# Two column blocks of the gate product at a time as seven half-size products (Strassen-Winograd) in a fused decoder layer

## The chip, the cores and the metric

One core of a Trainium2 chip runs the whole kernel as one program; the other cores are not used. The metric is the device time of one execution in microseconds. Every time in this document is of that program or of a variant of it with the same inputs.

## The reference, cut to what matters

One decoder layer on x, 512 rows of 1024, in float32. Three branches (dilated attention, a gated spatial mix, cross-attention into 256 memory rows) are each projected to 1024 channels, weighted by gates made from x, summed and projected once more; a gated MLP follows. The change is in the gates.

```python
gates = jax.nn.sigmoid((x @ w_gate + b_gate).astype(jnp.float32)).reshape(b_, s_, N_BRANCH, D_MODEL)
merged = (gates[:, :, 0] * (oa @ w_proj_a) + gates[:, :, 1] * (ob @ w_proj_b)
          + gates[:, :, 2] * (oc @ w_proj_c))
y = merged.astype(x.dtype) @ w_out
```

`w_gate` is 1024 x 3072: 24 column blocks of 128, eight to a branch.

## The kernel before, in words

**Products in three passes.** TensorE multiplies in a reduced float32 format. Every operand is therefore held as a high and a low part, and each product is made of three matmuls (`mm3`, L218 to L220): low weights with high data, high weights with low data, high with high. Each matmul loads its 128 x 128 weights anew. Nearly all matmuls stand at L220.

**The weight stream.** `add_load` (L99) lists the loads of weights, in the order of their use, and cuts each into units of up to 1024 columns. `emit_load` (L108) issues one load of up to 1 MB from SP's queue into one of three `raw` tiles. `emit_split` (L119) splits one unit: ScalarE writes the high part (`wh`, L133), VectorE the low part (`wl`, L134); there are four tiles of each (`wspl`). `unit()` (L141) hands out the next unit and first emits the splits of the two behind it and the loads of the two behind its own.

**The gates** (L780 to L795). For each of 24 blocks, a unit of 8 x 128 weights and 24 matmuls of 512 columns (8 row blocks of the weights, three passes) make `gate` in one PSUM bank; x stands transposed and split in `xTh` and `xTl`. ScalarE makes tanh of it (`gt`, L791). `merge` (L762) then multiplies the branch's projection for that block: 6 or 12 matmuls into `proj`, weights from a unit that serves four blocks (branches 0 and 2) or two (branch 1), and VectorE's L770, or L772 and L773, and in branch 2 also the split of the merged block (`mTh` L775, `mTl` L776). The merge of a block stands behind the gate matmuls of the next one (`late`).

**Beside it.** A generator, `side()` (L608), holds the attention, the spatial gating and the cross-attention in small steps; `fill()` (L621) takes one step, and stands behind every six gate matmuls. At the gates' start the spatial gating and the cross-attention are still to be done; they last into the first quarter of the gates.

**The order of the work.** The program text gives each instruction a priority. A scheduler, at compile time, sets the order in each engine's queue from these and from when operands and tiles should be ready, so that a later instruction can be put ahead of an earlier one; on the chip each engine runs its queue in order. Tiles come from pools: `big` (17 tiles of 8 KB a partition, `T8`), `work` (6 of 2 KB, `W2`), `raw` (3), `wspl` (4 and 4), PSUM (8 banks). An instruction that writes a new tile waits until one is free.

**After the gates.** `project` (L816) multiplies by `w_out`: two steps of 24 matmuls for all rows, then the last six steps for each row block in turn, with weights that `last_rows` (L798) splits into six `big` tiles (`lh`, `ll`). A norm, the MLP and a second norm follow.

Of the kernel before, what the change touches and what calls it, by code (L numbers as in the profile page):

```python
# [11 lines left out]
F32 = mybir.dt.float32  # L12
F32R = mybir.dt.float32r
AF = mybir.ActivationFunctionType
ALU = mybir.AluOpType
# [34 lines left out]
def bucket_rows():  # L50
    """Per dilation group the bucket (one-hot, rows 0-31) and the mask (row 32) of each diagonal."""
    rows = np.zeros((N_BUCKETS + 1, 3, VW), np.float32)
    for i in range(VW):
        for g in range(3):
            n = 255 - i if g == 0 else 127 - i
            if g == 0:
                ok, dist = 0 <= n <= 128, n
            elif g == 1:
                ok, dist = n >= 0, 4 * n
            else:  # L60
                ok, dist = n >= 0 and n % 4 == 0, 4 * n
            if ok:
                rows[int(bucket_of(np.array([dist]))[0]), g, i] = 1.0
            else:
                rows[N_BUCKETS, g, i] = NEG
    return rows
# [3 lines left out]
def layer_kernel(  # L70
# [8 lines left out]
    wspl = ctx.enter_context(tc.tile_pool(name="wspl", bufs=4))  # L79
    work = ctx.enter_context(tc.tile_pool(name="work", bufs=6))  # L80
    small = ctx.enter_context(tc.tile_pool(name="small", bufs=4))
# [11 lines left out]

    # ---------------------------------------------------------------- weight stream
    loads, prepared = [], {}
# [3 lines left out]
    def add_load(shape, src, parts):  # L99
        """One DMA of `shape`; parts: function raw -> list of (hi shape, raw view)."""  # L100
        n = len(loads)
        loads.append((shape, src))
        for f in parts:
            units.append((n, f))

    raws = {}

    def emit_load():  # L108
        n = state["load"]
        if n >= len(loads):  # L110
            return
        shape, src = loads[n]
        t = wraw.tile([P, 2048], F32, tag="raw", name=f"raw{n}")
        v = t[:, :shape[1] * shape[2]].rearrange("p (a b) -> p a b", a=shape[1])
        nc.sync.dma_start(v, src)
        raws[n] = v
        state["load"] += 1

    def emit_split():  # L119
        u = state["split"]  # L120
        if u >= len(units):
            return
        n, f = units[u]
        while state["load"] <= n:
            emit_load()
        src = f(raws[n])
        a = src.shape[1]
        h = wspl.tile([P, 1024], F32R, tag="wh", name=f"wh{u}")
        l = wspl.tile([P, 1024], F32R, tag="wl", name=f"wl{u}")
        size = a * src.shape[2]  # L130
        h3 = h[:, :size].rearrange("p (a b) -> p a b", a=a)
        l3 = l[:, :size].rearrange("p (a b) -> p a b", a=a)
        nc.scalar.activation(h3, src, AF.Copy)  # L133
        nc.vector.tensor_tensor(l3, src, h3.bitcast(F32), op=ALU.subtract)  # L134
        prepared[u] = (h3, l3)
        state["split"] += 1

    AHEAD = 2
    cursor = {"u": 0}

    def unit():  # L141
# [7 lines left out]
        return prepared.pop(u)  # L149

    def cols2(w, c0):
        src = w[:, c0:c0 + 256].rearrange("(k p) c -> p k c", p=P)
        add_load([P, 8, 256], src, [lambda r: r[:, :, 0:128], lambda r: r[:, :, 128:256]])

    def kcols(w, k0, nk, c0, nc_):
        """Rows k0*128.., a [128, nk, nc_] load in units of 1024 per partition."""
        src = w[k0 * P:(k0 + nk) * P, c0:c0 + nc_].rearrange("(k p) c -> p k c", p=P)
        per = 1024 // nc_
        parts = [lambda r, s=s: r[:, s:s + per, :] for s in range(0, nk, per)]
        add_load([P, nk, nc_], src, parts)  # L160
# [17 lines left out]
    kcols(wkv, 0, 8, 256, 256)  # L178
    for half in range(2):
        add_load([P, 2, 512], w_proj_a[0][:, half * 512:half * 512 + 512].rearrange("(k p) c -> p k c", p=P),  # L180
                 [lambda r: r])
        for j in range(2):
            cols2(wgate, half * 512 + 256 * j)
    for q in range(4):
        add_load([P, 4, 256], w_proj_b[0][:, q * 256:q * 256 + 256].rearrange("(k p) c -> p k c", p=P),
                 [lambda r: r])
        cols2(wgate, 1024 + q * 256)
    for half in range(2):
        add_load([P, 2, 512], w_proj_c[0][:, half * 512:half * 512 + 512].rearrange("(k p) c -> p k c", p=P),
                 [lambda r: r])  # L190
        for j in range(2):
            cols2(wgate, 2048 + half * 512 + 256 * j)
    def krows(w, k, split):
# [20 lines left out]
    def mm3_ops(ps, w, v, first, last):  # L214
        """ps += w.T @ v for operands split into (hi, lo)."""
        return ((ps, w[1], v[0], first, False), (ps, w[0], v[1], False, False), (ps, w[0], v[0], False, last))
# [11 lines left out]

    # ---------------------------------------------------------------- x, transposed and split
    xraw = []  # L230
# [39 lines left out]

    # ---------------------------------------------------------------- small parameters
    rows = const.tile([P, P], F32, name="rows")
# [60 lines left out]

    # ---------------------------------------------------------------- q, k, v
    qk12 = [T8(f"qk{i}") for i in range(2)]
# [85 lines left out]

    # ---------------------------------------------------------------- attention pieces
    NM = const.tile([P, 48], F32, name="NM")
# [3 lines left out]
    class Pair:  # L427
        """Two query blocks of one head: scores, softmax, weighted values (transposed)."""

# [7 lines left out]
        def score_ops(self):  # L437
            """Matmul arguments of the scores, in order."""
            part, h, pr = self.part, self.h, self.pr
# [80 lines left out]
    def alternate(a, b):  # L520
        """The matmuls of two heads in turn: they use different rows or columns of the array."""
        for pair in zip(a, b):
# [3 lines left out]
    def pipeline(groups):  # L526
        """groups: (part, first head, done); scores run two steps ahead of values."""
        items = [[Pair(part, h + i, pr) for i in range(2)] + [gi] for gi, (part, h, _) in enumerate(groups)
# [99 lines left out]

    # ---------------------------------------------------------------- gated spatial inputs, memory
    sgb = T8("sgb")  # L630
# [52 lines left out]
    kcT = [kct[:, i, :].rearrange("p (a c) -> p a c", a=2) for i in range(2)]  # L683
    vcN = T8("vcN")[:, 0, :].rearrange("p (a c) -> p a c", a=2)
    for j in range(2):
# [25 lines left out]
    nc.vector.tensor_copy(vcN, ps.rearrange("p (b c) -> p b c", b=2))  # L711
    ready.add("mix")

    # ---------------------------------------------------------------- spatial gating, cross-attention
    obT_h = T8("obTh", F32R)
# [32 lines left out]

    # ---------------------------------------------------------------- gates and branch projections
    m = [T8(f"m{i}") for i in range(2)]  # L750
# [27 lines left out]

    late = None
    for br, (nk, per, src) in enumerate(branches):  # L780
        for f in range(KD):
            if f % per == 0:
                wp = unit()
            w = unit()
            ps = bank("gate")
            for k in range(KD):
                mm3(ps, (w[0][:, k, :], w[1][:, k, :]), xs(k), k == 0, k == KD - 1)
                if k % 2 == 1:
                    fill()
            t = W2("gt")  # L790
            nc.scalar.activation(t, ps, AF.Tanh, bias=gb5[:, br * 8 + f:br * 8 + f + 1], scale=0.5)  # L791
            if late is not None:
                merge(*late)
            late = (br, f, t, wp)
    merge(*late)  # L795

    # ---------------------------------------------------------------- output projection, first norm
    def last_rows(n):  # L798
        """Split rows of the last LAST steps of a [*, 1024] weight, kept whole."""
        rows = []  # L800
# [15 lines left out]
    def project(nk, src, n, norm_in):  # L816
        """src (transposed, split) times the weight of the stream; norm_in(b) after each row block."""
        py = [[bank(f"y{b}{hf}") for hf in range(2)] for b in range(NB)]
# [64 lines left out]

    # ---------------------------------------------------------------- gated MLP
    h2 = [T8(f"h2_{i}", F32R) for i in range(NF // 2)]
# [36 lines left out]

    # ---------------------------------------------------------------- down projection, second norm
    lnp2 = T8("ln2").rearrange("p (k a) c -> p k (a c)", k=2)
# [25 lines left out]
```

## Time and profile before

| what | value |
|---|---|
| median of 3 runs | 822.16 us (822.1 to 822.8) |
| profiled execution, span from first to last instruction | 820.5 us |
| TensorE busy | 807.0 us (98%) |
| weight loads busy | 675.0 us (82%) |
| VectorE, ScalarE, GpSimd busy | 382.5, 284.4, 20.4 us |
| gates and projections | 211.5 to 405.3 us of the span |

The profiled execution is one run, and its own time is known by its span alone, 820.5 us; the median of the runs, 822.16, lies 1.7 us above it. An engine is busy in a row while one of its instructions is under way; TensorE's matmuls overlap, so their single durations add up to more than the time they take together, and the time of one is best read from the start of a run of them to the start of the next.

### The profile page before, as it was taken

To read this page: it belongs to the slowest core of one execution; us is meant where nothing else is said; L and a number is where in the kernel's file an instruction comes from. 1 tells how busy PE (TensorE), PEld (TensorE's weight loads), DVE (VectorE), ACT (ScalarE), POOL (GpSimd) and SP (SyncE) were. 2 spreads that over 40 slices of the span, in tenths; PEclk is the share of its full clock that TensorE was granted. 3 is DMA by queue.
4 is the path that set the end of the run, shared out by engine and by line. 5 is a ranking of instruction groups with operands and counts; after the bars stand their busy time and mean duration, and the time that the engine had idled before them with its cause. 6 is when DMAs were issued, how large, how long until landed. Compare 5 with 4: busy or idle time off the path is not lost.

```text
span 820.5 us, 9700 instructions
## 1 busy us (share of the span) xinstructions
PE 807.0 (98%) x4051; PEld 675.0 (82%) x4051; DVE 382.5 (47%) x591; ACT 284.4 (35%) x433; POOL 20.4 (2%) x32
## 2 busy tenths in 40 slices
PE   7999999999999999999999999999999999999996
PEld 6878997778877788888888988888888888888884
DVE  4333235836664334335856455544454445225055
ACT  4331246665365222223611243333333333224000
POOL 2001000100000000000000000000000000000000
PEclk9999999999999999999999999999999999999998
DMA  9355331122402133242840023233333324224002
GB/s 317 124 196 182 103 129 52 52 78 82 150 26 78 52 103 128 78 152 89 323 154 1 1 103 102 103 103 103 103 103 102 103 83 131 94 102 154 1 26 77
DMA packets 62411, 87.10 MB, mean 106 GB/s; under 512 B 1994, under 2 KB 50154, under 8 KB 62368
## 3 DMA queue, kind: packets, MB, share of 16 engines
q1 hardware_dynamic: 60960, 82.32, 29.5%
q0 software_dynamic: 1408, 4.17, 1.5%
q8 instruction: 32, 0.52, 0.3%
q14 instruction: 11, 0.09, 0.0%
HBM read 84.36 MB, written 4.47 MB: 108 GB/s over the span
## 4 chain that ended last, share of the span: by engine, by line
PE 98%; DMA 1%; DVE 0%; SPq 0%; issue 0%; DVEq 0%
PE y L220 20%; PE gate L220 16%; PE pa L220 13%; PE pb L220 13%; PE qk L220 7%; PE zb L220 6%; PE proj L220 5%; PE v L220 4%; PE up L220 3%; PE oT L524 1%; PE sc L524 1%; PE qc L220 1%; PE pt L493 1%; PE qk L362 1%; PE vc L220 1%; PE kc L220 1%
## 5 line engine op out<-in xcount | busy, mean ns | idle before, releaser
L134 DVE TENSOR_TENSOR wl<-raw,wh 128x1024 fp32r<-128x1024 f32 (+1 forms) x127 | 154.1, 1214 | 186.5 <-ACT wh L133 177.7
L133 ACT ACTIVATE wh<-raw 128x1024 fp32r<-128x1024 f32 (+1 forms) x127 | 133.2, 1050 | 192.9 <-PE pb L220 47.2
L220 PE MATMUL y<-wh,h 128*128 128x512 f32 x256 | 79.0, 389 | 0.0
L220 PE MATMUL gate<-xTh,wl 128*128 128x512 f32 x192 | 76.7, 400 | 0.0
L220 PE MATMUL gate<-xTh,wh 128*128 128x512 f32 x192 | 75.0, 390 | 0.0
L220 PE MATMUL gate<-xTl,wh 128*128 128x512 f32 x192 | 74.9, 390 | 0.0
L220 PE MATMUL pa<-hTh,wl 128*128 128x512 f32 x160 | 62.3, 389 | 0.0
L220 PE MATMUL pa<-hTl,wh 128*128 128x512 f32 x160 | 62.3, 389 | 0.0
L220 PE MATMUL pa<-hTh,wh 128*128 128x512 f32 x160 | 62.2, 389 | 0.0
L220 PE MATMUL pb<-hTh,wl 128*128 128x512 f32 x160 | 62.2, 389 | 0.0
L220 PE MATMUL pb<-hTl,wh 128*128 128x512 f32 x160 | 62.2, 389 | 0.0
L220 PE MATMUL pb<-hTh,wh 128*128 128x512 f32 x160 | 62.2, 389 | 0.0
L220 PEld LDWEIGHTS y<-wh,h 128*128 128x128 f32 x256 | 48.0, 188 | 10.1
L220 PE MATMUL y<-wl,h 128*128 128x512 f32 x128 | 49.8, 389 | 0.0
L898 DVE SCALAR_TENSOR_TENSOR c<-pa,par,c 128x511 f32<-128x511 f32 x20 | 15.0, 750 | 65.8 <-ACT c L897 65.8
L220 PEld LDWEIGHTS gate<-xTh,wl 128*128 128x128 f32 x192 | 36.1, 188 | 8.6 <-issue 1.2
L220 PEld LDWEIGHTS gate<-xTh,wh 128*128 128x128 f32 x192 | 36.0, 188 | 7.8
L897 ACT ACTIVATE c<-pa,par 128x512 f32<-128x512 f32 x20 | 15.6, 781 | 76.1 <-PE pa L220 76.1
L220 PEld LDWEIGHTS gate<-xTl,wh 128*128 128x128 f32 x192 | 36.1, 188 | 7.0
L220 PE MATMUL qk<-xTh,wl 128*128 128x512 f32 (+1 forms) x96 | 35.8, 374 | 0.0
L220 PE MATMUL qk<-xTh,wh 128*128 128x512 f32 (+1 forms) x96 | 35.7, 371 | 0.0
L220 PE MATMUL qk<-xTl,wh 128*128 128x512 f32 (+1 forms) x96 | 35.6, 372 | 0.0
(219 smaller groups left out, 1480.8 us busy)
## 6 DMA issues: line engine op xcount, KB each, us to landing
raw<-in_w_ffn_up SPq DMA_DIRECT2D x22, 1024.0 KB, 4.9
raw<-in_w_in SPq DMA_DIRECT2D x13, 1024.0 KB, 5.0
raw<-in_w_gate SPq DMA_DIRECT2D x12, 1024.0 KB, 5.0
raw<-in_w_ffn_down SPq DMA_DIRECT2D x11, 1024.0 KB, 4.7
raw<-in_w_out SPq DMA_DIRECT2D x4, 1024.0 KB, 4.7
shear<-vecs POOLq DMA_DIRECT2D x1, 2304.0 KB, 14.1
raw<-in_w_mem_kv SPq DMA_DIRECT2D x2, 1024.0 KB, 5.3
raw<-in_w_proj_b SPq DMA_DIRECT2D x4, 512.0 KB, 3.3
```

The source lines that it names most:

```text
L133: nc.scalar.activation(h3, src, AF.Copy)
L134: nc.vector.tensor_tensor(l3, src, h3.bitcast(F32), op=ALU.subtract)
L220: nc.tensor.matmul(ps, w, v, start=first, stop=last)
L362: nc.tensor.matmul(ps[:, sl], w[a][:, k, :], xs(k0 + k, sl)[c], start=k0 + i + k == 0, stop=k0 > 0 and i == 2 and k == 3)
L493: nc.tensor.transpose(pt[:, kb, u, :], self.p[:, u, kb * P:(kb + 1) * P], ident)
L524: nc.tensor.matmul(ps, w, v, start=first, stop=last)
L897: nc.scalar.activation(c, pa, AF.Identity, bias=CB(i), scale=CW(2, i))
L898: nc.vector.scalar_tensor_tensor(c[:, 1:], pa[:, :S - 1], CW(1, i), c[:, 1:], op0=ALU.mult, op1=ALU.add)
```

## The change

Blocks 0 to 3 of branch 0 stay. From block 4 on, two neighbouring blocks f and f + 1 are made together. Their weights are a 2 x 2 matrix of quarters (rows 0 to 511 and 512 to 1023 of w_gate; columns of f and of f + 1), a11, a12, a21, a22, of 4 x 128 x 128 each; x is a 2 x 2 matrix of quarters too (the same halves of its channels; rows 0 to 255 and 256 to 511). Winograd's form of Strassen's method makes the 2 x 2 product from seven products of quarters instead of eight, with sums of quarters.

- **Sums of x** (`data_sums`): made once, ahead of the gates, on GpSimd (5 instructions of 1024 columns) and VectorE (3), then split (4 on ScalarE, 4 on VectorE) into four `big` tiles that live until the last group.
- **Sums of weights**: for each load, three GpSimd instructions of 512 columns when it has landed (two into a tile of the new pool `wsum`, one in place), and a fourth in place once the load's first unit is split.
- **Units**: four a group instead of two: a11 and a12; the two sums; a11 - a21 and a22; the quarter a12 less a sum (512 columns).
- **Products** (`Seven`): each is 4 x 3 = 12 matmuls of 256 columns. In order: 1 (unit 1, into x), 2 (unit 1, into y), 3 (unit 2, added to x), 4 (unit 2, into z), 5 (unit 3, added to x), then the late merges of the group before, 6 (unit 3, added to x), 7 (unit 4, added to z). x has a PSUM bank, y and z share one. ScalarE copies x after products 1, 3 and 5; VectorE adds these copies to y and z into the two `gt` tiles after products 2, 5 and 7; ScalarE makes tanh in three parts. `fill()` stands behind each product.
- **Room**: `vcN` moves from `big` to `const`, `work` has 7 tiles, and the scratch for DMAs that GpSimd issues is set to 4096.

```diff
-    work = ctx.enter_context(tc.tile_pool(name="work", bufs=6))
+    wsum = ctx.enter_context(tc.tile_pool(name="wsum", bufs=2))
+    work = ctx.enter_context(tc.tile_pool(name="work", bufs=7))
...
+        if n in seven_loads:
+            s = wsum.tile([P, 2, 512], F32, tag="sums", name=f"sums{n}")
+            s2, s1 = [s[:, i, :].rearrange("p (k c) -> p k c", k=4) for i in range(2)]
+            a11, a21, a22 = v[:, 0:4, 0:P], v[:, 0:4, P:2 * P], v[:, 4:8, P:2 * P]
+            nc.gpsimd.tensor_tensor(s1, a21, a22, op=ALU.add)
+            nc.gpsimd.tensor_tensor(s2, s1, a11, op=ALU.subtract)
+            nc.gpsimd.tensor_tensor(a21, a11, a21, op=ALU.subtract)
+            sums[n] = s
...
+        if n in seven_loads and a == 8 and n not in halved:
+            halved.add(n)
+            a12 = raws[n][:, 4:8, 0:P]
+            nc.gpsimd.tensor_tensor(a12, a12, sums[n][:, 0, :].rearrange("p (k c) -> p k c", k=4),
+                                    op=ALU.subtract)
...
+    def seven_cols(src):
+        n = len(loads)
+        seven_loads.add(n)
+        add_load([P, 8, 256], src, [lambda r: r[:, :, 0:P], lambda r: sums[n],
+                                    lambda r: r[:, :, P:2 * P], lambda r: r[:, 4:8, 0:P]])
...
+    class Seven:
+        def __init__(self, raw, sums_, out1, out2, step=lambda: None):
+            self.raw, self.sums, self.step = raw, sums_, step
+            xx, yz = bank("xx"), bank("yz")
+            self.x, self.y, self.z = xx[:, 0:256], yz[:, 0:256], yz[:, 256:512]
+            self.cu = W2("cu")
+            self.u3 = W2("u3")[:, 0:256]
+            self.out1, self.out2 = out1, out2
+        def product(self, ps, w, src, kk, half, first=True):
+            hi, lo = src
+            ts = slice(256 * half, 256 * half + 256)
+            for k in range(4):
+                v = hi[kk][:, k, ts], lo[kk][:, k, ts]
+                for i, (pp, ww, vv) in enumerate(((ps, w[1], v[0]), (ps, w[0], v[1]), (ps, w[0], v[0]))):
+                    nc.tensor.matmul(pp, ww(k), vv, start=first and k + i == 0, stop=k == 3 and i == 2,
+                                     skip_group_check=not first)
+            self.step()
...
+        def p1(self):
+            self.u0 = unit()
+            self.product(self.x, self.part(self.u0, 0, False), self.raw, 0, 0)
+            nc.scalar.activation(self.cu[:, 0:256], self.x, AF.Copy)
+        def rest(self):
+            self.product(self.y, self.part(self.u0, 1, False), self.raw, 1, 0)
+            nc.vector.tensor_tensor(self.out1[:, 0:256], self.cu[:, 0:256], self.y, op=ALU.add)
+            u1 = unit()
+            self.product(self.x, self.part(u1, 0, True), self.sums, 1, 1, first=False)
+            nc.scalar.activation(self.cu[:, 256:512], self.x, AF.Copy)
+            self.product(self.z, self.part(u1, 1, True), self.sums, 0, 0)
+            self.u2, self.u3w = unit(), unit()
+            self.product(self.x, self.part(self.u2, 0, False), self.sums, 0, 1, first=False)
+            nc.scalar.activation(self.u3, self.x, AF.Copy)
+            nc.vector.tensor_tensor(self.out2[:, 256:512], self.u3, self.z, op=ALU.add)
+        def finish(self):
+            self.product(self.x, self.part(self.u2, 1, False), self.sums, 1, 0, first=False)
+            self.product(self.z, self.part(self.u3w, 0, False), self.raw, 1, 1, first=False)
+            nc.vector.tensor_tensor(self.out1[:, 256:512], self.cu[:, 256:512], self.z, op=ALU.add)
+            return self.x
+    def data_sums(hi, lo, eng):
+        f = [T8("tf") for _ in range(2)]
+        for kk in range(2):
+            for hf in range(2):
+                s = slice(2 * hf, 2 * hf + 2)
+                eng[hf].tensor_tensor(f[kk][:, s, :], hi[kk][:, s, :].bitcast(F32), lo[kk][:, s, :].bitcast(F32),
+                                      op=ALU.add)
+        q = [[f[kk][:, :, 256 * t:256 * t + 256] for t in range(2)] for kk in range(2)]
+        eng[0].tensor_tensor(q[0][0], q[0][1], q[0][0], op=ALU.subtract)
+        eng[1].tensor_tensor(q[0][1], q[1][1], q[0][1], op=ALU.subtract)
+        eng[0].tensor_tensor(q[1][1], q[1][1], q[0][0], op=ALU.subtract)
+        eng[0].tensor_tensor(q[1][0], q[1][0], q[1][1], op=ALU.subtract)
...
+    xsums = data_sums(xTh, xTl, (nc.gpsimd, nc.vector))
...
-        for f in range(KD):
+        for f in range(0, KD, 2):
             if f % per == 0:
                 wp = unit()
...
+            ts = [W2("gt") for _ in range(2)]
+            blk = Seven((xTh, xTl), xsums, ts[0], ts[1], fill)
+            blk.p1()
+            blk.rest()
+            merge_late()
+            first = blk.finish()
+            nc.scalar.activation(ts[1][:, 0:256], first, AF.Tanh, bias=gate_bias(br, f + 1), scale=0.5)
+            nc.scalar.activation(ts[1][:, 256:512], ts[1][:, 256:512], AF.Tanh, bias=gate_bias(br, f + 1), scale=0.5)
+            nc.scalar.activation(ts[0], ts[0], AF.Tanh, bias=gate_bias(br, f), scale=0.5)
+            late += [(br, f + i, ts[i], wp) for i in range(2)]
...
-    nc = bacc.Bacc("TRN2", target_bir_lowering=False, num_devices=1)
+    nc = bacc.Bacc("TRN2", target_bir_lowering=False, num_devices=1, dynamic_dma_scratch_size=4096)
```

## Rows read from the trace of the kernel before

**Rows 1.** Page: span; busy us, share of the span, instructions.

```profile
span 820.5 us, 9700 instructions
...
PE 807.0 (98%) x4051; PEld 675.0 (82%) x4051; DVE 382.5 (47%) x591; ACT 284.4 (35%) x433; POOL 20.4 (2%) x32
```

**Rows 2.** Page: granted TensorE clock in 40 slices, in tenths.

```profile
PEclk9999999999999999999999999999999999999998
```

**Rows 3.** Page: the chain that ended last, by engine and by line.

```profile
PE 98%; DMA 1%; DVE 0%; SPq 0%; issue 0%; DVEq 0%
PE y L220 20%; PE gate L220 16%; PE pa L220 13%; PE pb L220 13%; PE qk L220 7%; PE zb L220 6%; PE proj L220 5%; PE v L220 4%; PE up L220 3%; PE oT L524 1%; PE sc L524 1%; PE qc L220 1%; PE pt L493 1%; PE qk L362 1%; PE vc L220 1%; PE kc L220 1%
```

**Rows 4.** The chain in order of time: start us, us, what.

```profile
205.77 5.76 PE vc L220 x48
...
213.80 4.09 PE gate L220 x18
217.89 2.59 PE sv L724 x12
...
307.41 5.44 PE gate L220 x24
312.85 2.72 PE proj L220 x12
...
461.04 14.39 PE up L220 x120
```

**Rows 5.** Windows: the gates' stretch; busy us (count) by engine, PEclk, DMA share.

```profile
211.50:405.30 193.80, 193.80 (x922) 157.20 (x921) 90.97 (x129) 71.49 (x112) 0.00 (x0) 1.00 0.33 113
```

**Rows 6.** Groups of instructions, shapes kept apart, whole span: VectorE.

```profile
L134 DVE TENSOR_TENSOR wl<-raw,wh 128x1024 fp32r<-128x1024 f32 x125 | 152.7, 1223 | 180.0 <-ACT wh L133 171.1 <-PE tm L677 8.6
...
L773 DVE TENSOR_TENSOR m<-m,gt 128x512 f32<-128x512 f32 x16 | 11.0, 688 | 0.3
...
L134 DVE TENSOR_TENSOR wl<-raw,wh 128x512 fp32r<-128x512 f32 x2 | 1.4, 687 | 6.6 <-ACT wh L133 6.6
...
L225 DVE TENSOR_TENSOR kcT<-kc,kcT 128x256 fp32r<-128x256 f32 x2 | 0.8, 414 | 0.0
```

**Rows 7.** Groups, shapes kept apart: ScalarE, the first row in the gates' stretch.

```profile
L133 ACT ACTIVATE wh<-raw 128x1024 fp32r<-128x1024 f32 x31 | 32.7, 1056 | 39.3 <-PE gate L220 34.3 <-PE proj L220 4.6 <-PE vc L220 0.4
...
L791 ACT ACTIVATE gt<-gate,gb 128x512 f32<-128x512 f32 x24 | 16.4, 684 | 47.7 <-PE gate L220 46.5 <-PE oT L524 1.2
...
L133 ACT ACTIVATE wh<-raw 128x512 fp32r<-128x512 f32 x2 | 1.3, 628 | 4.9 <-DMA raw<-in_w_in 4.9
...
L223 ACT ACTIVATE kcT<-kc 128x256 fp32r<-128x256 f32 x2 | 0.8, 380 | 0.1
```

**Rows 8.** Groups, shapes kept apart, whole span: GpSimd's only two-input instruction.

```profile
L649 POOL TENSOR_TENSOR mv<-mv,mhalf 128x1 f32<-128x1 f32 x12 | 11.2, 932 | 739.2 <-DVE mv L648 739.2
```

**Rows 9.** DMA issues to landing; GpSimd's issues by time; first reader of `bias`.

```profile
raw<-in_w_gate SPq DMA_DIRECT2D x12, 1024.0 KB, 5.0
...
bias<-shear POOLq DMA_DIRECT2D x2, 256.0 KB, 6.2
...
62.97 1.50 POOL L312 DMA_DIRECT2D bias<-shear  x2
...
L475 DVE CUSTOM_DVE_ANT_0 p<-sc,bias x32: 274/418/425, 118.5 to 171.4; 128x256 f32<-128x256 f32 x28, 128x128 f32<-128x128 f32 x4
```

More of the change, by code (lines that the diff above doesn't have):

```diff
@@ L106, in layer_kernel @@
     raws = {}
+    seven_loads, halved, sums = set(), set(), {}
     def emit_load():
@@ L178, in layer_kernel @@
     kcols(wkv, 0, 8, 256, 256)
[L179 to L192, printed above, removed]
+    PER = (4, 2, 4)
+    wprojs = (w_proj_a[0], w_proj_b[0], w_proj_c[0])
+    for br in range(3):
+        for f in range(0, KD, 2):
+            if f % PER[br] == 0:
+                cs = slice(f * P, (f + PER[br]) * P)
+                add_load([P, 1024 // (PER[br] * P), PER[br] * P],
+                         wprojs[br][:, cs].rearrange("(k p) c -> p k c", p=P), [lambda r: r])
+            c0 = br * D + f * P
+            if br == 0 and f < 4:
+                cols2(wgate, c0)
+            else:
+                seven_cols(wgate[:, c0:c0 + 256].rearrange("(k p) c -> p k c", p=P))
     def krows(w, k, split):
@@ L227, in split_of, with part @@
             nc.vector.scalar_tensor_tensor(lo, src, scale, hi.bitcast(F32), op0=ALU.mult, op1=ALU.subtract)
+    class Seven:
[15 more added lines that the diff above has]
+            self.step()
+        @staticmethod
+        def part(u, half, wide):
+            if wide:
+                return tuple((lambda k, t=t: t[:, half, k * P:(k + 1) * P]) for t in u)
+            return tuple((lambda k, t=t: t[:, 4 * half + k, :]) for t in u)
+        def p1(self):
[18 more added lines that the diff above has]
+            return self.x
@@ new lines, in data_sums @@
+    def data_sums(hi, lo, eng):
[10 more added lines that the diff above has]
+        eng[0].tensor_tensor(q[1][0], q[1][0], q[1][1], op=ALU.subtract)
+        th = [T8(f"th{kk}", F32R) for kk in range(2)]
+        tl = [T8(f"tl{kk}", F32R) for kk in range(2)]
+        for kk in range(2):
+            for hf in range(2):
+                s = slice(2 * hf, 2 * hf + 2)
+                split_of(th[kk][:, s, :], tl[kk][:, s, :], f[kk][:, s, :])
+        return th, tl
@@ L683, in layer_kernel @@
     kcT = [kct[:, i, :].rearrange("p (a c) -> p a c", a=2) for i in range(2)]
-    vcN = T8("vcN")[:, 0, :].rearrange("p (a c) -> p a c", a=2)
+    vcN = const.tile([P, S], F32, name="vcN").rearrange("p (a c) -> p a c", a=2)
     for j in range(2):
@@ L777, in merge, with gate_bias, merge_late @@
                                            op0=ALU.mult, op1=ALU.subtract)
-    late = None
+    def gate_bias(br, f):
+        return gb5[:, br * 8 + f:br * 8 + f + 1]
+    late = []
+    def merge_late():
+        for args in late:
+            merge(*args)
+        late.clear()
     for br, (nk, per, src) in enumerate(branches):
-        for f in range(KD):
+        for f in range(0, KD, 2):
             if f % per == 0:
                 wp = unit()
[L784 to L795, printed above, removed]
+            if br == 0 and f < 4:
+                for ff in (f, f + 1):
+                    w = unit()
+                    ps = bank("gate")
+                    for k in range(KD):
+                        mm3(ps, (w[0][:, k, :], w[1][:, k, :]), xs(k), k == 0, k == KD - 1)
+                        if k % 2 == 1:
+                            fill()
+                    t = W2("gt")
+                    nc.scalar.activation(t, ps, AF.Tanh, bias=gate_bias(br, ff), scale=0.5)
+                    merge_late()
+                    late.append((br, ff, t, wp))
+                continue
+            ts = [W2("gt") for _ in range(2)]
+            blk = Seven((xTh, xTl), xsums, ts[0], ts[1], fill)
+            blk.p1()
+            blk.rest()
+            merge_late()
+            first = blk.finish()
[3 more added lines that the diff above has]
+            late += [(br, f + i, ts[i], wp) for i in range(2)]
+    merge_late()
     def last_rows(n):
```

## The prediction

> **What bounds the kernel now.** I read the page's busy shares first. TensorE is busy for 807.0 of 820.5 us, its weight loads for 82%, VectorE for 47%, ScalarE for 35% and GpSimd for 2% [rows 1]; the reader should see one full engine and three with room. The granted clock stands in its top tenth, 2.4 GHz, in all but the last slice [rows 2], so no stretch is slow for want of clock. Next the chain that ended last: it lies on TensorE for 98%, 16% of it in `gate` and 5% in `proj` [rows 3]. Then the chain in order of time, which gives what one matmul costs from start to start. The "mean ns" of a matmul row is no use here, since neighbours overlap: 192 gate matmuls of 400 ns would not fit beside the others. Divided out, 24 gate matmuls of 512 columns take 5.44 us, or 226.7 ns each; 120 matmuls of 256 columns in `up` take 14.39 us, or 119.9 ns, and 48 in `vc` take 5.76 us, or 120.0 ns [rows 4]. So a matmul of half the width costs 53% of a whole one, not 50%. Last, the gates' own stretch, 211.5 to 405.3 us: TensorE is busy for all of its 193.8 us, VectorE for 91.0, ScalarE for 71.5, GpSimd for none [rows 5]. So TensorE's matmul time is what ends the stage, and anything that shortens it is a gain as long as the other three keep up.
>
> **What it removes and adds on TensorE.** Four column blocks stay as they are; 20 become ten groups of two. Two blocks were 48 matmuls of 512 columns: 48 x 226.7 ns = 10.88 us. A group is seven products of 4 rows of weights x 3 passes = 84 matmuls of 256 columns: 84 x 119.9 ns = 10.07 us. That is 0.81 us saved a group, **8.1 us** for ten. The multiplications fall by an eighth, but most of it is paid back in the dearer half-width matmul. All of this lies on the path. The nearest rows for the price agree within 0.1 ns [rows 4], so its bounds are narrow.
>
> The Trainium skill ("TensorE: Matmul & The Clock Gate", section "Back-to-back issue gap") gives N/2.4 + 2.5 ns for the isolated matmul at the full clock, 215.8 ns for 512 columns and 109.2 for 256. This trace shows 226.7 and 119.9, about 11 ns more at either width; by the page's figures the saving would be 480 x 215.8 - 840 x 109.2 ns = 11.9 us. The rows decide.
>
> **What it adds elsewhere, per group.** Splits: three units of 1024 and one of 512 in place of two of 1024. On VectorE that is 3 x 1.223 + 0.69 (a two-input 512-wide row) = 4.36 us for 2.45 [rows 6]. Three additions out of PSUM, 256 wide, at the 414 ns of the 256-wide row [rows 6] are 1.24. So VectorE gets 3.15 us more a group and 31.5 in all. On ScalarE the splits rise by 1.056 + 0.628, three 256-wide copies are 3 x 0.380, and the tanh is cut in three instead of two (at most 0.1): 2.9 a group [rows 7]. The sums of x, made once, are 7 VectorE instructions of 1024 (8.6 us), 4 on ScalarE (4.2) and 5 on GpSimd. With these VectorE is at 91.0 + 31.5 + 8.6 = 131 and ScalarE at 71.5 + 29 + 4.2 = 105 of 186 us: neither becomes the bound on average.
>
> GpSimd has no addition of this width in the trace. Its only row is the power on one column, 932 ns [rows 8]; from below I take VectorE's 0.69 us for 512, from above 0.932 us and 512 columns at VectorE's slope ((1223 - 688)/512 = 1.04 ns each), 1.47 us. I take 1.47, as it rests on the engine's own row. Four a group are 5.9 us, and the five of 1024 some 2.0 each: 40 x 1.47 + 10 = 69 of 186 us. It is not the bound either.
>
> **What waits where.** TensorE runs its queue in order, so each product needs its operand in time. Within a group, products 1, 3, 5 and 6 accumulate into one PSUM tile that ScalarE copies after 1, 3 and 5. Copies 1 and 3 (0.38 us) have a product of 12 x 119.9 ns = 1.44 us between; copy 5 has the late projections, 12 or 24 matmuls, 2.72 us or twice that [rows 4]. At 0 each; without that cover 0.4 us and a hand-over. Product 4 writes the bank that VectorE reads after product 2, and has product 3 as cover.
>
> The splits have less room. `wspl` holds four tiles each of high and low halves; already ScalarE's splits wait 34.3 us for `gate` matmuls to free one [rows 7]. A group needs four units beside the projection's own, which stays held until its late merge. Where two projection units are held (all of branch 1, and the first group of each projection half elsewhere), unit 3 can be split only after product 2 and is needed two products later: 1.056 + 1.223 = 2.28 of 2.88 us, 0.6 to spare for the hand-overs. At six group boundaries the next group's first unit gets its tile only after product 6, with product 7's 1.44 us as cover for 2.28: 0.84 us and hand-overs short, at most 6 us for all. I take 0 for these: the late projections need nothing but their weights, and the scheduler does draw ready matmuls forward: in the trace 18 gate matmuls run in a row and then 12 of `sv`, while the program text asks for 6 of the one after a step of the other [rows 4].
>
> What no scheduler's order can know is GpSimd. If VectorE and GpSimd hinder each other, a split comes late by anything from 0 to 1.47 us. GpSimd is busy 37% of the stage (69 of 186); a split that meets a running sum waits half of it, 0.73 us on average: 0.37 x 0.73 = 0.27. One split a group (unit 3's) has no room for it: **+0.3 us a group, 3 us in all**, bounds 0 and 14.7.
>
> Edits at nothing: the sums of x stand at the gates' start, 211.5 us, and are first needed by the third product of the first group, behind four whole blocks, at least 4 x 5.44 = 21.8 us later; without that cover VectorE's 8.6 us. The larger set of long-lived tiles leaves the last rows of the output weight no room until the sums of x are done; their six splits (6 x 1.223 = 7.3 us on VectorE) then lie under the last projections and the first 48 output matmuls, 2.72 + 10.9 us; without cover 7.3. The smaller scratch slows GpSimd's DMA issues at most: `bias` lands 6.2 us after 63 us and is first read at 118.5 [rows 9], so 49 us may be lost there free. Bytes stay the same; a gate load lands in 5.0 us [rows 9], and each is issued more than a group (10 us) ahead, so GpSimd's wait for it blocks only later sums. `work` gets one buffer and a group holds up to six of seven, so the tail of the cross-attention may be put off; gate matmuls take its place.
>
> **The sum.** Span 820.5 - 8.1 + 3 = 815.4 us. The median is 822.16, 1.7 above the profiled span, with the same taken for after: **817.0 us**.
>
> **The rivals.**
> (a) The splits keep up, and nothing is given back: 822.16 - 8.1 = 814.0. For it: VectorE has 55 us to spare in the stage. Chance 0.10, with 0.02 of it for a cheaper 256-wide matmul, which would give some 4 us more than the rows do. That is the rate of the TensorE page of the Trainium skill, cited above; the rows speak against it.
> (b) Waits of 0.65 to 0.97 us a group eat the gain: within 0.2% (1.6 us, about what a measurement of this kernel can tell from no change), 820.5 to 823.8. Chance 0.15.
> (c) Slower: VectorE reads two SBUF operands in every split and GpSimd two in every sum; if one shuts the other out for a whole instruction, the place is the low half of unit 3, which stands behind one sum in each group, 1.47 us, with no room left: 10 x 1.47 = 14.7, less 8.1: 828.8. It decides from 0.81 us a group on. For it: GpSimd's three sums come in a row when a load lands. Against: locked shares add up to 69 us and some 90 of VectorE (42 large splits of 1.223, ten small, the 16 sums of `m` and what follows), 159 of 186, so most splits find a gap. Chance 0.25. The Trainium skill ("SBUF — State Buffer", section "Who interferes with whom") states just this: a VectorE instruction with two SBUF inputs contends with a GpSimd one that reads SBUF, and the second to issue blocks. No row here shows it, GpSimd being idle in the stage.
> (d) The sums of x stand in VectorE's queue, wait there for GpSimd's and hold up the spatial gating: 8.6 us once, 822.16 - 8.1 + 3 + 8.6 = 825.7. Chance 0.05.
> A change that does not do what it says would show as 48 wide matmuls where 84 narrow ones should be; I give it nothing.
>
> **How the numbers follow.** My forecast, a small part given back (815 to 820.5), has 0.45; with (a) faster has 0.55, (b) 0.15, (c) and (d) 0.30. The range goes from 812.5, a little under (a), to 828, just short of (c)'s full price: outside lie the worst of (c) and the cheap matmul of (a), under 0.2. The likeliest case's own range is 815 to 820.5.
>
> **What would show it.** Right: 480 gate matmuls of 512 columns gone, 840 of 256 columns at 120 ns from start to start; runs of 12 of them without a gap in the chain; gates to the end of the last projection in 186 to 190 us. The 3 us would show as pieces of TensorE idle, or matmuls further apart, ahead of product 5, released by VectorE's split. Wrong: splits on VectorE longer than 1.22 us in the mean (rival c), a gap between 211 and 250 us (rival d), waits before products 3 or 4 that name ScalarE's copy, or matmuls of 256 columns away from 120 ns.

## The result, and the profile after

The changed kernel takes **834.53 us** (median of 4 runs, 833.7 to 835.51) against 822.22 us for the kernel before (4 runs, 822.1 to 822.8): ratio 1.015, 95% interval 1.0138 to 1.0162. It is slower by 12.3 us; 817.0 was forecast, with 828 as the upper end. The page of the profiled execution of the changed kernel (span; busy us, share and count; granted clock in tenths; the chain by engine):

```profile
span 832.3 us, 10664 instructions
...
PE 803.2 (97%) x4411; PEld 686.7 (83%) x4411; DVE 443.1 (53%) x648; ACT 319.2 (38%) x497; POOL 102.2 (12%) x77
...
PEclk9999999999999999999999999999999999999998
...
PE 92%; DVE 4%; ACT 2%; DMA 1%; issue 1%; SPq 0%; DVEq 0%; ACTq 0%
```

TensorE is busy for 4 us less than before [rows 1] in a span 12 us longer, at the same granted clock [rows 2], so it waits some 16 us more. The chain says for whom: 98% of it lay on TensorE [rows 3], now 92%, with VectorE and ScalarE for the rest. Windows of the changed kernel (busy us and count of PE, PEld, DVE, ACT, POOL; clock; DMA share; GB/s), from the gates' start to the first group of seven, and from there to the end of the gates:

```profile
211.00:253.40 42.40, 38.16 (x210) 30.76 (x209) 38.03 (x56) 23.00 (x46) 17.89 (x9) 1.00 0.20 62
253.40:420.60 167.20, 155.59 (x1092) 141.70 (x1091) 109.13 (x132) 82.84 (x131) 54.99 (x33) 1.00 0.32 107
```

TensorE is idle for 4.2 us in the first and for 11.6 in the second, where it never was before [rows 5]. The waits of the changed kernel's gates that end on a matmul (total us, times, longest; `sv` and `gate` belong to the opening, `xx` to the groups):

```profile
PE xx L274 <- DVE wl L145: 7.3, 6, 1.7
...
PE xx L274 <- ACT u L298: 4.3, 9, 0.6
...
PE sv L825 <- DVE ws L430: 3.2, 1, 3.2
...
PE gate L243 <- DVE wl L145: 1.1, 1, 1.1
```

Six waits for the low half of a split, nine for ScalarE's copy after product 5: 11.6 us, all of the idle time inside the groups. One group of branch 1 in the chain in order of time of the changed kernel (start, us, what). The pieces are products 3 and 4, a projection, product 5, ScalarE's copy `u`, product 6, the two halves of a split, and then products 1 and 2 of the next group, a projection and so on. Product 7, `yz`, has no piece behind product 6, since what is waited for next does not depend on it:

```profile
308.46 1.43 PE xx L274 x12
309.90 1.44 PE yz L274 x12
311.34 2.75 PE proj L243 x12
314.08 1.44 PE xx L274 x12
...
315.55 0.39 ACT u L298
...
315.99 1.72 PE xx L274 x12
...
317.78 1.07 ACT wh L144
...
318.87 1.24 DVE wl L145
...
320.15 1.69 PE xx L274 x12
321.84 1.44 PE yz L274 x12
323.28 2.75 PE proj L243 x12
326.03 1.43 PE xx L274 x12
...
331.65 1.44 PE xx L274 x12
```

A product of 12 half-width matmuls takes 1.43 to 1.44 us: 120 ns each, as in [rows 4]. From one group's product 5 (314.08) to the next one's (331.65) it is 17.57 us; 84 x 119.9 ns and 24 projection matmuls of 226.7 ns are 15.51. The 2.06 us lie in two places. Product 6 (315.99) stands right behind product 5 and waits for the copy between them, 0.47 us. Then product 1 of the next group (320.15) waits for its weights: their high half can start only when product 6 has given a tile back, at 317.78, and 1.07 + 1.24 us outlast product 7 by 1.0 us. After each wait a run of 12 takes 1.69 to 1.72 us, so a wait costs some 0.26 us on top. Fifteen of these with the 11.6 us make an estimated 15.5; less the 8.1 saved, plus 4.2 at the opening, that is 11.6 of the 11.8 us by which the span grew.

### The profile page after: what moved, and what is told of

Its sections match the earlier page's. It is cut to its first block, busy times and chain, and to the rows that moved or that the text cites. A ratio compares the mean times of both kernels' runs of the same rounds, so it can differ in the third digit from the quotient of the medians.

```text
span 832.3 us, 10664 instructions
## 1 busy us (share of the span) xinstructions
PE 803.2 (97%) x4411; PEld 686.7 (83%) x4411; DVE 443.1 (53%) x648; ACT 319.2 (38%) x497; POOL 102.2 (12%) x77
## 4 chain that ended last, share of the span: by engine, by line
PE 92%; DVE 4%; ACT 2%; DMA 1%; issue 1%; SPq 0%; DVEq 0%; ACTq 0%
PE y L243 20%; PE pa L243 13%; PE pb L243 13%; PE qk L243 7%; PE xx L274 7%; PE zb L243 6%; PE proj L243 5%; PE yz L274 4%; PE v L243 4%; PE up L243 3%; PE gate L243 2%; DVE wl L145 2%; PE oT L624 1%; PE sc L624 1%; PE qc L243 1%; PE pt L593 1%
## 5 line engine op out<-in xcount | busy, mean ns | idle before, releaser
L145 DVE TENSOR_TENSOR wl<-raw,wh 128x1024 fp32r<-128x1024 f32 (+1 forms) x137 | 170.4, 1244 | 161.9 <-ACT wh L144 153.1
L144 ACT ACTIVATE wh<-raw 128x1024 fp32r<-128x1024 f32 (+1 forms) x137 | 139.6, 1020 | 191.6 <-PE pb L243 47.2
L749 POOL TENSOR_TENSOR mv<-mv,mhalf 128x1 f32<-128x1 f32 x12 | 11.4, 956 | 507.8 <-DVE mv L748 507.8
L274 PE MATMUL xx<-th,wl 128*128 128x256 f32 x120 | 35.0, 291 | 4.3 <-ACT u L298 4.3
L1023 DVE TENSOR_TENSOR c<-c,pb 128x512 f32<-128x512 f32 x20 | 13.8, 688 | 40.5 <-PE pb L243 40.5
L243 PEld LDWEIGHTS pa<-hTl,wh 128*128 128x128 f32 x160 | 30.0, 188 | 6.3
L243 PEld LDWEIGHTS pa<-hTh,wh 128*128 128x128 f32 x160 | 30.1, 188 | 6.2
L243 PEld LDWEIGHTS pb<-hTh,wl 128*128 128x128 f32 x160 | 30.1, 188 | 6.2
## 6 DMA issues: line engine op xcount, KB each, us to landing
shear<-vecs POOLq DMA_DIRECT2D x1, 2304.0 KB, 14.7
```

Source lines behind the costliest of these rows:

```text
L243: nc.tensor.matmul(ps, w, v, start=first, stop=last)
L274: nc.tensor.matmul(pp, ww(k), vv, start=first and k + i == 0, stop=k == 3 and i == 2, skip_group_check=not first)
L749: nc.gpsimd.tensor_tensor(dst, dst, mhalf, op=ALU.pow)
L1023: nc.vector.tensor_tensor(c, c, pb, op=ALU.mult)
```

## The experiments

Eleven more kernels, each timed beside the kernel before on the same chip: e1 to e4 on one chip, e5 to e8 on a second, e9 to e11 on a third, where the kernel before had 822.08, 822.13 and 821.92 us. e1 to e4 leave out a part of the computation, so that its price shows; none of them is a version to use. Three theories are tried: A, a missing tile for the splits makes TensorE wait in the groups; B, GpSimd's sums hold up VectorE's splits there; C, the sums of x hold up the opening of the gates.

"First group" is the start of the first product of seven; the kernel before starts the same block at 248.8 us. "Clock" is the granted clock from 205 to 249 us, as a share of 2.4 GHz; before the change it is 1.00.

| run | what is changed | us | ratio to before (95%) | first group at | clock |
|---|---|---|---|---|---|
| the change | | 834.53 | 1.015 (1.0138 to 1.0162) | 253.2 | 1.00 |
| e1 | no sums of weights | 834.5 | 1.0151 (1.0135 to 1.0167) | 254.5 | 0.96 |
| e2 | no sums of x | 829.74 | 1.0099 (1.0083 to 1.0116) | 248.4 | 1.00 |
| e3 | neither | 828.35 | 1.0076 (1.0061 to 1.0091) | 248.2 | 1.00 |
| e4 | neither, five split tiles | 817.82 | 0.9947 (0.9932 to 0.9962) | 249.9 | 1.00 |
| e5 | five split tiles | 825.02 | 1.0038 (1.0027 to 1.005) | 254.4 | 0.96 |
| e6 | own projections | 826.78 | 1.0055 (1.004 to 1.007) | 255.2 | 0.96 |
| e7 | sums of x later | 836.6 | 1.0184 (1.0163 to 1.0204) | 255.0 | 0.96 |
| e8 | five tiles, own projections, later | 817.5 | 0.9943 (0.9929 to 0.9958) | 252.2 | 1.00 |
| e9 | five tiles, own projections | 820.31 | 0.9983 (0.9974 to 0.9993) | 254.8 | 0.96 |
| e10 | e8, sums of x on VectorE alone | 824.34 | 1.0028 (1.0017 to 1.0039) | 258.9 | 0.93 |
| e11 | e10, sums of weights on VectorE too | 827.11 | 1.0074 (1.0047 to 1.0102) | 260.3 | 0.92 |

**e1, no sums of weights.**

```diff
-            nc.gpsimd.tensor_tensor(s1, a21, a22, op=ALU.add)
-            nc.gpsimd.tensor_tensor(s2, s1, a11, op=ALU.subtract)
-            nc.gpsimd.tensor_tensor(a21, a11, a21, op=ALU.subtract)
...
-        add_load([P, 8, 256], src, [lambda r: r[:, :, 0:P], lambda r: sums[n],
+        add_load([P, 8, 256], src, [lambda r: r[:, :, 0:P], lambda r: r[:, :, 0:P],
```

> Leaves out the sums of weights (all 40 GpSimd instructions of the groups; the second unit is split from the raw weights instead), so GpSimd does nothing beside VectorE in the groups. Theory A (tiles: the next group's first unit finds no free split tile before product 6, and product 6 has nothing left to hide the copy after product 5): the period of a branch 1 group stays at about 17.5 us against 15.5 of matmuls, and the time falls from 834.5 by 0 to 4 us, to 830 to 834. Theory B (GpSimd and VectorE shut each other out, and late splits are the loss): the period falls to 15.5 to 16, the time by 10 us or more, to 824 or less. Theory C (the opening with the sums of x) says nothing on the groups and leaves the 4 us ahead of the first group.

The time did not move: 834.5 us. Between 255 and 420 us, the large splits on VectorE of the changed kernel:

```profile
L145 DVE TENSOR_TENSOR wl<-raw,wh 128x1024 fp32r<-128x1024 f32 x27 | 37.5, 1390 | 25.6 <-ACT wh L144 25.5
L145 DVE TENSOR_TENSOR wl<-sums,wh 128x1024 fp32r<-128x1024 f32 x9 | 17.7, 1970 | 5.4 <-ACT wh L144 5.4
```

and of e1:

```profile
L136 DVE TENSOR_TENSOR wl<-raw,wh 128x1024 fp32r<-128x1024 f32 x37 | 45.3, 1224 | 32.8 <-ACT wh L135 32.8
```

The waits of e1 that end on a matmul:

```profile
PE xx L260 <- DVE wl L136: 6.1, 6, 1.0
...
PE xx L260 <- ACT u L284: 4.3, 9, 0.6
```

GpSimd does hold VectorE: a split takes 1.39 us in the mean, that of the sums 1.97, and without GpSimd's sums 1.22 as in [rows 6]. But the same 6 and 9 waits are there without it, 10.4 us of the 11.6. The 1.2 us won at the boundaries went again at the opening (254.5 for 253.2), and there it is TensorE's clock that took them. The first matmuls behind the opening's wait for `ws`, in the changed kernel and then in e1:

```profile
222.05 2.86 PE L825 MATMUL sv<-vg,ws 128*128 128x256 f32 x12 [3.17 <-DVE ws L430]
```

```profile
221.56 4.52 PE L811 MATMUL sv<-vg,ws 128*128 128x256 f32 x12 [3.13 <-DVE ws L416]
```

and the window 223 to 225 us of e1, with the granted clock as the third number from the end:

```profile
223.00:225.00 2.00, 2.00 (x6) 1.57 (x5) 2.00 (x4) 0.00 (x0) 0.00 (x0) 0.50 0.00 0
```

In e1 the clock stood at 0.50, the level of 1.2 GHz, and the same 12 matmuls took 1.66 us longer; in the changed kernel it stayed at 1.00 behind the same wait. So theory B falls as the main cause, with 1.2 us of idle to its name.

**e2, no sums of x, and e3, neither.**

```diff
-    xsums = data_sums(xTh, xTl, (nc.gpsimd, nc.vector))
+    xsums = xTh, xTl
```

> Leaves out the sums of x (the groups read x itself in their place), keeps the sums of weights. Theory C (the 12 instructions at the gates' start hold VectorE's queue, 4.2 us of idle TensorE between 211 and 253 us): the first group starts 4 us earlier and the time falls to about 830. If the opening is lost for another reason, for want of work tiles or through the first sums of weights, the time stays within 1 us of 834.5. Theories A and B expect the groups themselves unchanged, 16 us over their matmuls.

> Leaves out both kinds of sums, so GpSimd is idle in the gates as before the change; four split tiles of each kind as in the change. Theory A: the waits at the group boundaries stay, and the time is 825 to 829, still above the kernel before. Theory B: with GpSimd gone the saving of 8 us shows, 813 to 817. A reading between the two is the share of each.

e2 gave 829.74 us, 4.8 less, and its first group starts at 248.4: the opening's loss is the sums of x. e3, with this edit and that of e1, gave 828.35: with no GpSimd instruction in the gates at all, the kernel is still 6 us slower than before. At e2's and e3's openings the clock stayed at 1.00, so this pair prices the sums of weights with four tiles: about 1.4 us. VectorE's queue at the opening of the changed kernel (start, us):

```profile
204.63 2.35 DVE L314 TENSOR_TENSOR tf<-xTh,xTl 128x1024 f32<-128x1024 f32 x2
206.90 2.89 DVE L248 TENSOR_TENSOR oaT<-w,oaT 128x512 fp32r<-128x512 f32 x1
...
215.58 3.05 DVE L145 TENSOR_TENSOR wl<-raw,wh 128x1024 fp32r<-128x1024 f32 x1
218.56 2.84 DVE L248 TENSOR_TENSOR oaT<-w,oaT 128x512 fp32r<-128x512 f32 x1
221.32 1.28 DVE L430 TENSOR_TENSOR ws<-wsT,maskT 128x512 f32<-128x512 f32 x2
```

with GpSimd's at the same time:

```profile
205.99 3.25 POOL L317 TENSOR_TENSOR tf<-tf 128x1024 f32<-128x1024 f32 x1 [18.35 <-DVE tf L314]
215.14 2.41 POOL L319 TENSOR_TENSOR tf<-tf 128x1024 f32<-128x1024 f32 x1 [5.90 <-DVE tf L318]
217.63 3.22 POOL L320 TENSOR_TENSOR tf<-tf 128x1024 f32<-128x1024 f32 x1
```

A 512-wide instruction that takes 0.69 us elsewhere [rows 6] takes 2.89 and 2.84, each ending 0.55 us behind GpSimd's, and the masked weights of the spatial gating (`ws`), for which TensorE waits 3.2 us, stand behind them.

**e4, neither, with a fifth split tile.**

```diff
-    wspl = ctx.enter_context(tc.tile_pool(name="wspl", bufs=4))
+    wspl = ctx.enter_context(tc.tile_pool(name="wspl", bufs=5))
```

> As the run without both kinds of sums, with five split tiles of each kind instead of four (the room is that of the sums). Theory A: the next group's first unit is split before product 6 and the waits at the boundaries go, 5 to 10 us less than the run with four: 816 to 822. Theory B: no change against the run with four, within 1 us.

817.82 us against 828.35 with four: **10.5 us** for one tile more of each half. The only wait of e4's groups that still ends on a matmul:

```profile
PE xx L260 <- ACT u L284: 1.4, 3, 0.5
```

None for a low half is left, where e3 has the same six and nine as e1, and of the nine for the copy three remain: other matmuls now stand where they hide it. That settles theory A.

**e5, the whole change with five split tiles.**

```diff
-    big = ctx.enter_context(tc.tile_pool(name="big", bufs=17))
+    big = ctx.enter_context(tc.tile_pool(name="big", bufs=16))
...
-    wspl = ctx.enter_context(tc.tile_pool(name="wspl", bufs=4))
+    wspl = ctx.enter_context(tc.tile_pool(name="wspl", bufs=5))
```

> The whole change with five split tiles of each kind instead of four; the room comes from one of the 17 big tiles. Theory A (a missing fifth tile is the loss in the groups): as in the pair of runs without sums, about 10 us less than the change, 822 to 826. Rival B2 (with both kinds of sums running, VectorE's splits are held by GpSimd, 1.39 and 1.97 us for 1.22, so that a fifth tile helps less): 828 to 832. Big tiles one fewer: nothing, or some us at the opening or at the output projection if a tile is missed there.

825.02 us, 9.5 less. Against e4 it keeps 7.2 us of loss. The first group starts at 254.4 instead of 249.9, so 4.5 of it is the opening: a wait of 3.5 us for `ws`, and behind it a lower clock as in e1. The 2.7 left is what both kinds of sums cost beyond it; two waits for a low half, 1.5 us, are still there.

**e6, own projections.** Each group's own two projections stand between its products 5 and 6, so that a projection unit is given back within its group.

```diff
             blk.rest()
             merge_late()
+            pps = [proj_mm(br, f + i, wp) for i in range(2)]
             first = blk.finish()
...
-            late += [(br, f + i, ts[i], wp) for i in range(2)]
+            for i in range(2):
+                evac(br, f + i, ts[i], pps[i])
```

> Each group's own projections stand between its products 5 and 6, instead of those of the group before; four split tiles. In branch 1 only one projection unit is held at a time then, so the next group's first unit can be split before product 6. Theory A: the wait for the low half goes at the boundaries and the copy after product 5 is covered if the scheduler leaves the projections there: 824 to 829. If it is not the held unit but the number of splits in a row on ScalarE and VectorE that makes the first unit late, the time stays at 833 to 836.

826.78 us, 7.8 less than the change, with four tiles, though the opening lost 2 us more (255.2, with a lower clock as in e1). The only wait of e6's groups that ends on a matmul:

```profile
PE xx L274 <- ACT u L298: 4.6, 7, 1.3
```

No wait for a low half is left. This frees a tile by order instead of by room, and does most of what the fifth tile does.

**e7, sums of x later.**

```diff
-    xsums = data_sums(xTh, xTl, (nc.gpsimd, nc.vector))
...
             if br == 0 and f < 4:
+                if f == 2:
+                    xsums = data_sums(xTh, xTl, (nc.gpsimd, nc.vector))
```

> The sums of x stand two gate blocks further on in the program text (ahead of block 2 instead of ahead of block 0), otherwise the change. Theory C (they hold VectorE's queue just when the attention's end and the spatial gating wait on it): 3 to 5 us less, 829.5 to 831.5, with the first group starting at about 249 us. If the sums cost the same wherever they stand: 834 to 835.

A miss: 836.6 us, 2 us more. The gates now start undisturbed, but the sums meet the cross-attention's softmax. VectorE's queue in e7:

```profile
230.97 6.15 DVE L314 TENSOR_TENSOR tf<-xTh,xTl 128x1024 f32<-128x1024 f32 x2
...
245.73 4.31 DVE L585 TENSOR_SCALAR p<-p,RD 128x256 f32<-128x256 f32 x4
```

The two sums take 6.15 us for 2.35 above, beside GpSimd's own two; TensorE waits 5.1 us for the rescaled `p`, and behind this wait the clock falls to 0.50. The profiled execution is the longest of e7's four (840.0 us); its clock fell again behind two of the waits between groups, of 1.7 us each.

**e8, all three, and e9, without the later place.** The edits are those of e5, e6 and, for e8, e7.

```diff
             merge_late()
+            pps = [proj_mm(br, f + i, wp) for i in range(2)]
...
-    wspl = ctx.enter_context(tc.tile_pool(name="wspl", bufs=4))
+    wspl = ctx.enter_context(tc.tile_pool(name="wspl", bufs=5))
```

> All three together, five split tiles, own projections, sums of x two blocks later; the whole computation. Theories A and C: nearly all of the 8.1 us of matmul time shows, 815 to 819, faster than the kernel before. Theory B2 (GpSimd's hold on VectorE becomes the limit once the tiles suffice): 820 to 826.

> Five split tiles and own projections, with the sums of x where the change has them. The run with the sums two blocks later had 817.5 us. If the later place helps once the tiles suffice (first group at 252.2 us against 253.4 to 255.2 in the runs with the early place): 818.5 to 821. If it makes no difference, or hurts as it did alone (836.6 against 834.5): 815 to 817.5.

e8 is the best version: **817.5 us**, ratio 0.9943 (0.9929 to 0.9958), faster than both kernels, with the whole computation. Seven products and a projection of its chain in order of time, in branch 1:

```profile
314.10 2.87 PE xx L274 x24
316.97 1.44 PE yz L274 x12
318.41 1.44 PE xx L274 x12
319.85 1.44 PE yz L274 x12
321.29 1.44 PE xx L274 x12
322.73 1.44 PE yz L274 x12
324.17 2.75 PE proj L243 x12
```

No engine but TensorE stands in it, and from the first group to the end of the gates TensorE is never idle:

```profile
252.20:414.00 161.80, 161.80 (x1134) 148.97 (x1133) 114.92 (x147) 88.32 (x143) 52.87 (x33) 1.00 0.37 128
```

e9 has 820.31: here the later place is worth 2.8 us, though by itself (e7) it lost 2. Part of the 2.8 is the clock. In e9 TensorE waits 3.5 us for `ws`, and the 12 matmuls behind it take 4.52 us at a clock of 0.50, as in e1; in e8 the waits add up to 2.1 us and the clock stays at 1.00. In e8 TensorE waits 2.1 us for `p`, not 5.1 as in e7. Why the sums fall so differently in the two queues was not traced further.

**e10 and e11, the sums on VectorE.**

```diff
-                    xsums = data_sums(xTh, xTl, (nc.gpsimd, nc.vector))
+                    xsums = data_sums(xTh, xTl, (nc.vector, nc.vector))
...
-            nc.gpsimd.tensor_tensor(s1, a21, a22, op=ALU.add)
+            nc.vector.tensor_tensor(s1, a21, a22, op=ALU.add)
```

The second part, for all four sums of weights, is in e11 alone.

> Five split tiles, own projections, sums of x two blocks later and all on VectorE (12 instructions of 1.22 us); the weight sums stay on GpSimd. If what the opening loses is the hold of GpSimd's sums on VectorE (2 sums of x took 6.15 us there for 2.35, four rescalings of 256 columns 4.31 for 1.4), the first group starts nearer to 249 us than to 252 and the time falls by 1 to 3 us to 814.5 to 816.5. If VectorE's own load is the loss, it stays at 817.5 or rises by some 3 us, as five more instructions of 1.22 lie on VectorE.

> As the run before, with the weight sums on VectorE too (40 instructions of 512 columns, 0.69 us each, 27.5 us in all on VectorE); GpSimd is idle in the gates. Theory B2 (GpSimd costs more through its hold on VectorE than its work would cost there): the time is that of the run before or up to 2 us less, 813 to 816.5. If GpSimd takes real work off VectorE, VectorE's 27.5 us more show in part: 818 to 824.

824.34 and 827.11 us, both above what was expected. The wait at the opening of e8 and of e10:

```profile
PE pt L593 <- DVE p L585: 2.1, 3, 1.3
```

```profile
PE pt L593 <- DVE p L585: 7.5, 1, 7.5
```

The first group moves to 258.9 and 260.3, 6.7 and 8.1 us later than in e8, which is all of e10's 6.8 us and most of e11's 9.6. In e10, 5.4 us of it is the longer wait, as the sums stand ahead of the rescaled `p` in VectorE's queue, and the rest goes with the clock, which stood at 0.50 from 243 to 249 us. So the sums' time on VectorE hurts ahead of the first group, and GpSimd, for all its hold, takes work off it: theory B2 falls too.

## Why the prediction was wrong

**Right: the saving.** 84 matmuls of 256 columns at 120 ns; in e8 nothing else is on the chain in branch 1. There the span is 816.1 us, 4.4 less than before, although the first group starts 3.4 us later, so the groups gave 7.8 of the 8.1 forecast.

**The average loads: right that none is the bound.** ScalarE was put at 105 us in the gates; the two windows have 105.8. VectorE was put at 131 and has 147.2: its 43 large splits took 67.0 us in these windows, 14.4 more than at 1.223 each, and that is GpSimd's hold. A 512-wide GpSimd sum was put at 1.47 us; in the quiet it takes 1.28 to 1.30 (e2 and e8 show many), and the means over the changed kernel are 1.43 to 2.08, as VectorE holds it in turn:

```profile
L127 POOL TENSOR_TENSOR raw<-raw 128x512 f32<-128x512 f32 x10 | 20.8, 2079 | 0.0
L126 POOL TENSOR_TENSOR sums<-sums,raw 128x512 f32<-128x512 f32 x10 | 16.8, 1677 | 0.8
```

**The step that failed: "I take 0 for these".** The prediction saw the place: at six group boundaries the next first unit gets its tile only after product 6, 0.84 us and hand-overs short, "at most 6 us for all". There were six, 7.3 us of idle and about 0.26 us more at each restart, 8.9. It was set to 0 because the late projections "need nothing but their weights" and can be drawn forward into a gap. They were drawn forward, but not to the boundary: in the chain they stand behind products 2 and 4, and none was left behind product 7. One supply of ready matmuls was counted as cover for two places at once. Why the scheduler put them there is not shown; ScalarE's next split waits for a tile at either place too. And as they left the place between products 5 and 6, the copy there lost its cover, "at 0 each; without that cover 0.4 us and a hand-over": nine times, 4.3 us and 2.3 for the restarts. e4 and e6 show the cause from two sides, by a tile more and by a tile given back earlier.

**An edit at nothing that was not: the sums of x.** Their cover was counted for their own readers, four blocks on. What they delayed was what stood behind them in VectorE's queue, the attention's last splits and the spatial gating's mask: 4.8 us by e2.

**The other terms.** The 0.3 us a group for GpSimd's hold was right in kind: the splits grew by 0.17 to 0.75 us. At four tiles it was worth 1.4 us (e3 against e2) of the 3 forecast, as TensorE mostly waited for the tile anyway. The rows of the output weight, the smaller scratch and the work tiles cost nothing that shows: from 420.6 to 487.1 us, the output projection and the first of the MLP, TensorE is busy for all of the 66.5 us.

**The rivals.** (c) had the sign, and the hold that it names is real, but it is 1.4 us and not 14.7. (d) had the mechanism of the opening at nearly twice the price, 8.6 us for 4.8. The loss of 12.3 us is mostly (d) and the waits for tiles and copies together, which no rival had.

## What to carry to other kernels

When a product is cut into more units of weights per microsecond, count the tiles of the ring again: for each unit, from whose last matmul its tile comes and how much matmul time lies between that and its own first use, with every unit that is held across groups counted in. Work that can fill a gap is a stock: subtract it where it is used first, and see what its old place was covering. Work moved in front of a stage costs what stands behind it in the queue, not only what reads it. And before a difference of a microsecond or two is put down to an edit, compare the granted clock of the same stretch in both runs.

## What the runs showed of the hardware that was not expected

VectorE and GpSimd hold each other up by as much as a whole instruction. A 1024-wide split takes 2.27 us beside a GpSimd sum, 1.22 alone; a 512-wide one 2.89 for 0.69; GpSimd's 512-wide sums 2.0 to 2.3 us for 1.29. The split of 2.27 us in the changed kernel, with the sum beside it:

```profile
320.24 1.30 POOL L151 TENSOR_TENSOR raw<-raw,sums 128x512 f32<-128x512 f32 x1 [10.43 <-DVE wl L145]
320.34 2.27 DVE L145 TENSOR_TENSOR wl<-sums,wh 128x1024 fp32r<-128x1024 f32 x1
```

It started 0.1 us behind the sum and took 1.05 longer than usual; the sum lost nothing. The Trainium skill ("SBUF — State Buffer", section "Who interferes with whom") says that of two such instructions the second to issue blocks; this pair agrees. The same section of the Trainium skill also names `tensor_scalar` among the operations that can enter a two-port mode and then contend. In e7 four such rescalings, with one tensor input of 256 columns, took 4.31 us together beside GpSimd's sums, against 0.35 each in the kernel before; that fits, though no row shows the mode.

A gap on TensorE costs more than the gap: in the changed kernel's groups a run of 12 half-width matmuls takes 1.69 to 1.72 us after one, and 1.43 to 1.45 behind other gate or projection matmuls, at an unchanged granted clock of 1.00 of 2.4 GHz. Behind the cross-attention's small matmuls it takes 1.60 to 1.63 without any gap.

Behind a gap the clock can fall, too. Behind waits of 3.1 to 7.9 us at the opening of e1, e5 to e7 and e9 to e11 the granted clock fell to 0.50, that is from 2.4 to 1.2 GHz, for some microseconds, and 12 matmuls took up to 4.52 us for 2.86. In e7 it fell behind two waits of 1.7 us between groups too. Behind 3.2 us in the changed kernel it did not fall; no run shows what decides.
